# A hybrid attention layer: the compressed branch with queries as the stationary operand, and its values in one block-diagonal product

## The chip, the cores and the metric

The kernel runs on one core of one Trainium2 chip. The metric is the device time of one execution in microseconds. The unchanged kernel took 315.85 us in the median of three executions (315.37 to 315.9). A profiled execution of it took 316.46 us.

## The reference

One decoder layer on 512 tokens of width 1024. After an RMS norm that is modulated by a condition, one projection makes queries, keys, values and gates for two groups of eight heads of width 64. Group A is attention over a window of 128 with a sink per head. Group B (two key groups g, four heads r in each) adds up three branches over the same queries: a compressed one, a selected one and a window of 512. In the compressed branch 31 overlapping blocks of 32 tokens are mapped to one key and one value each, and all 512 queries attend to those that have ended:

```python
def compress_blocks(t, pos, w1, w2):
    ...
    return jax.nn.silu(flat @ w1) @ w2

    logits_c = jnp.einsum('btgrd,bngd->bgrtn', qi, kc)
    p_c = masked_softmax(logits_c, c_end[None, :] <= t[:, None])
    o_cmp = jnp.einsum('bgrtn,bngd->btgrd', p_c, vc)
    ...
o_b = gb[..., 0, :] * o_cmp + gb[..., 1, :] * o_sel + gb[..., 2, :] * o_win
y = concat(o_a * silu(z_a), o_b * silu(z_b)) @ w_out ;  x + gate * y
```

With SEL_TOPK = 16 and only eight blocks of 64, the selected branch takes every earlier block, so it is plain causal attention with its own keys and values.

## The kernel before

Everything is float32 to the outside. A projection is split in a high part (fp32r, which TensorE multiplies in one pass) and the rest (low): three one-pass products high x high, high x low, low x high make one full product. A product of plain float32 operands takes two passes, and each pass shows as a matmul of its own in the profile. The function `split` makes the parts of a weight tile: ScalarE copies the high part (L175), VectorE subtracts (L176). `unit_nat` (L473) projects with tokens on partitions, `unit_col` (L483) with output columns on partitions; a unit of L483 is 24 products of 512 columns, eight steps of three.

Attention of a head pair (g = 0 and 1 with the same r) goes in slots of 128 queries. A slot has scores (L869, or L843 where the first query block takes both branches at once), mask and bias on VectorE (L874, L845), exponential on ScalarE (L881, L850), scaling on VectorE (L902), transposes on TensorE through two PSUM banks called pt (L917, L927), a copy on ScalarE (L918, L928), and the products with values (L944), which collect all four query blocks of one r in one PSUM bank, po. Group A's 16 slots come first, then seven slots for each r of group B. Scores use two PSUM banks called s. The query tiles qs hold high parts in 64 partitions and low parts in the other 64, so a contraction over 128 partitions adds both (L533 on ScalarE, L534 on VectorE).

The compressed branch lies beside that. `cmp_mlp` makes kc and vc (L602 to L648; L631 multiplies the value half). `cmp_attn` makes scores of all queries (L660), with kTc, 32 block keys, as the stationary operand and 512 queries moving: one product for each head, its 32 result rows in one quarter of the PSUM partitions, so that four heads of a group lie in one bank (s for g = 0, pj for g = 1). Since softmax wants queries on partitions, ScalarE copies each bank (L665), TensorE transposes it in four blocks (L669), and VectorE adds the mask (L671). Maximum, subtraction, exponential, sum, gate and scaling follow for two query blocks at a time (L678 to L688). Then the probabilities are transposed back (L695), copied (L697), and `slot_pv` adds for each r and g a product over 32 partitions to the bank po (L950).

What order the engines work in is set by two things. The program writes slots and a stream of side work alternately: `run` advances the stream by a given number of microseconds after each slot, and the stream (`gen1`, `gen2`) yields an estimated cost after each step, between projection steps and between the pieces of `posts`, in which `cmp_mlp` and `cmp_attn` stand. Then a scheduler orders the instructions of each engine by their dependencies and a model of durations. Only what stands in a `block()` keeps its order on TensorE. On the chip each engine runs its own row of instructions in order, so the first that waits holds up all behind it. In `gen2` the side work is eight z units (L483) and four gate slices (L704 on VectorE). The output projection (L483 with yh, yl) ends the program.

Of the kernel before, what the change touches and what calls it, by code (L numbers as in the profile page):

```python
# [81 lines left out]
def hybrid_layer_kernel(ctx, tc, A, out):  # L82
# [31 lines left out]
    rest = con.tile([128, 960], F32, name="rest")  # L114
# [3 lines left out]
    cmask = rest[:, 832:960].rearrange("p (a b) -> p a b", a=NB)  # L118
    qga, kga, qgb, kgs, kgw, kgc = (sml[:, 64 * i:64 * i + 64] for i in range(6))
# [335 lines left out]
    def PT():  # L455
        return ps_t.tile([128, 512], F32, name="pt")
# [40 lines left out]
    qs = {}  # L497
# [96 lines left out]
    def cmp_mlp():  # L594
# [23 lines left out]
        sTv = W2("csTv", (128, 2, 2, 4, 32))  # L618
        ptv = pt[:, 0:256].rearrange("p (c n) -> p c n", c=2)
        ACT.activation(sT, ptv[:, :, 0:64], AF.Copy, scale=0.5)  # L620
        for hc in range(2):
            DVE.tensor_scalar(sTv[:, hc], ptv[:, hc, 64:128].rearrange("p (g n) -> p g n", g=2)[:, :, None, :]
                              .to_broadcast([128, 2, 4, 32]), 0.5, None, op0=OP.mult)
# [5 lines left out]
        for g in range(2):  # L629
            for hc in range(2):  # L630
                PE.matmul(pv[:, 64 * g:64 * g + 64], sTv[:, hc, g].rearrange("p r n -> p (r n)"), w2[:, 1, hc, :],  # L631
                          start=hc == 0, stop=hc == 1)
        for g in range(2):
            vc[g] = mp.tile([128, HD], F32, name=f"vc{g}")
            ACT.activation(vc[g], pv[:, 64 * g:64 * g + 64], AF.Copy)
# [11 lines left out]
        kTc = mp.tile([128, 2, 32], F32, name="kTc")  # L647
        DVE.tensor_copy(kTc.rearrange("p g n -> p (g n)"), pt[:, 0:64])  # L648
# [3 lines left out]
    def cmp_attn():  # L652
        kTc = X["kTc"]
        L = [mp.tile([128, 2, 257], F32, name="pa", bufs=3).rearrange("p a b -> p (a b)")[:, 0:512]
             .rearrange("p (a b c) -> p a b c", a=2, b=2) for _ in range(2)]
        pss = [ps_s.tile([128, 512], F32, name="s"), PJ()]
        with block():
            for g in range(2):
                for r in range(4):
                    PE.matmul(pss[g][32 * r:32 * r + 32, :], kTc[:, g, :], qs[8 + 4 * g + r].bitcast(F32),  # L660
                              start=True, stop=True)
        for g in range(2):
            ps = pss[g]
            st_ = W2("cst")
            ACT.activation(st_.rearrange("p (i q) -> p i q", i=NB), rev(ps.rearrange("p (i q) -> p i q", i=NB)), AF.Copy)  # L665
            yield 0.95
            pt = PT()
            for i in range(NB):
                PE.transpose(pt[:, 128 * i:128 * i + 128], st_[:, 128 * i:128 * i + 128], ident)  # L669
# [435 lines left out]
```

## Time and profile before

| | |
|---|---|
| median of three executions | 315.85 us |
| the profiled execution | 316.46 us |
| its span, first to last instruction | 314.7 us |
| TensorE busy | 306.3 us (97%) |
| VectorE busy | 237.3 us (75%) |
| ScalarE busy | 195.5 us (62%) |
| granted TensorE clock, mean | 0.995 |

A matmul's record lasts from its start to the modelled end of its results, so records of neighbours overlap: 512-wide products start some 0.23 us apart and each is recorded with 0.40 us. What a product costs TensorE is therefore read from the distance of starts, or from the chain of waits, where 18 of them take 4.20 us. The chain follows the work that ended last back to what released it.

### The profile page before, as it was taken

To read this page: it belongs to the slowest core of one execution; us is meant where nothing else is said; L and a number is where in the kernel's file an instruction comes from. 1 tells how busy PE (TensorE), PEld (TensorE's weight loads), DVE (VectorE), ACT (ScalarE), POOL (GpSimd) and SP (SyncE) were. 2 spreads that over 40 slices of the span, in tenths; PEclk is the share of its full clock that TensorE was granted. 3 is DMA by queue.
4 is the path that set the end of the run, shared out by engine and by line. 5 is a ranking of instruction groups with operands and counts; after the bars stand their busy time and mean duration, and the time that the engine had idled before them with its cause. 6 is when DMAs were issued, how large, how long until landed. Compare 5 with 4: busy or idle time off the path is not lost.

```text
span 314.7 us, 5828 instructions
## 1 busy us (share of the span) xinstructions
PE 306.3 (97%) x2122; PEld 252.9 (80%) x2123; DVE 237.3 (75%) x658; ACT 195.5 (62%) x472; POOL 5.1 (2%) x22
## 2 busy tenths in 40 slices
PE   7999999999999999999999999999999999999995
PEld 3678878788988899889873878788788878788885
DVE  5579999999966658898996998988686687544221
ACT  6486448668966674767917767788785877503000
POOL 0000000002000000000000000000000000000000
PEclk9799999999999999999999999999999999999999
DMA  7999948800491809070653004222420220253201
GB/s 268 373 407 409 402 163 253 294 2 0 111 326 26 277 6 277 29 260 2 200 174 130 0 2 133 69 67 70 134 69 0 69 67 3 67 167 109 93 33 69
DMA packets 28232, 44.12 MB, mean 140 GB/s; under 512 B 1787, under 2 KB 19612, under 8 KB 28204
## 3 DMA queue, kind: packets, MB, share of 16 engines
q1 hardware_dynamic: 26908, 41.57, 39.0%
q10 hardware_dynamic: 1296, 2.18, 2.2%
q8 instruction: 17, 0.28, 0.4%
q14 instruction: 11, 0.09, 0.1%
HBM read 41.61 MB, written 2.14 MB: 139 GB/s over the span
## 4 chain that ended last, share of the span: by engine, by line
PE 77%; DVE 12%; DMA 4%; ACT 3%; issue 2%; SPq 0%; POOL 0%; DVEq 0%; ACTq 0%; POOLq 0%
PE pj L483 29%; PE sq L291 7%; PE po L944 7%; PE s L869 7%; PE pj L473 7%; PE pt L927 4%; PE skv L292 4%; DMA raw<-in_w_gate 3%; PE pt L917 3%; PE s L602 3%; DVE qs L534 2%; DVE kTb L552 1%; DVE wl L176 1%; PE po L950 1%; DVE raw L704 1%
## 5 line engine op out<-in xcount | busy, mean ns | idle before, releaser
L175 ACT ACTIVATE wh<-raw 128x512 fp32r<-128x512 f32 (+1 forms) x52 | 31.2, 636 | 13.5 <-PE pj L483 13.4
L176 DVE TENSOR_TENSOR wl<-raw,wh 128x512 fp32r<-128x512 f32 (+1 forms) x52 | 34.8, 690 | 5.2 <-ACT wh L175 3.5
L473 PE MATMUL pj<-wh,hh 128*128 128x256 f32 (+1 forms) x128 | 37.0, 289 | 0.0
L473 PE MATMUL pj<-wl,hh 128*128 128x256 f32 (+1 forms) x128 | 36.7, 287 | 0.1
L473 PE MATMUL pj<-wh,hl 128*128 128x256 f32 (+1 forms) x128 | 36.5, 285 | 0.0
L881 ACT ACTIVATE pp<-pp,nm 128x256 f32<-128x256 f32 (+2 forms) x48 | 29.3, 612 | 6.6 <-DVE nm L874 6.3
L483 PE MATMUL pj<-hh,wh 128*128 128x512 f32 x80 | 32.1, 402 | 0.0
L483 PE MATMUL pj<-hh,wl 128*128 128x512 f32 x80 | 32.0, 400 | 0.0
L483 PE MATMUL pj<-hl,wh 128*128 128x512 f32 x80 | 31.9, 398 | 0.0
L874 DVE CUSTOM_DVE_ANT_0 pp<-s,bias 128x256 f32<-128x256 f32 (+2 forms) x48 | 25.5, 551 | 3.6 <-PE s L869 3.5
L483 PE MATMUL pj<-yl,wh 128*128 128x512 f32 (+1 forms) x72 | 26.6, 372 | 0.0
L483 PE MATMUL pj<-yh,wh 128*128 128x512 f32 (+1 forms) x72 | 26.6, 371 | 0.0
L483 PE MATMUL pj<-yh,wl 128*128 128x512 f32 (+1 forms) x72 | 26.4, 369 | 0.0
L1032 DVE SCALAR_TENSOR_TENSOR fin<-pj,gate,xr 128x512 f32<-128x512 f32 (+1 forms) x9 | 6.2, 691 | 25.1 <-PE pj L483 25.1
L473 PEld LDWEIGHTS pj<-wl,hh 128*128 128x128 f32 x128 | 24.1, 188 | 0.4 <-DVE wl L176 0.3
L473 PEld LDWEIGHTS pj<-wh,hh 128*128 128x128 f32 x128 | 24.1, 188 | 0.3 <-issue 0.2
L473 PEld LDWEIGHTS pj<-wh,hl 128*128 128x128 f32 x128 | 24.1, 188 | 0.2 <-issue 0.2
L869 PE MATMUL s<-kTb,qs 128*128 128x256 f32 (+2 forms) x96 | 23.5, 356 | 0.0
L902 DVE TENSOR_SCALAR pp<-pp,rr,grev 128x256 f32<-128x256 f32 (+2 forms) x48 | 21.1, 476 | 0.7
L928 ACT COPY ptT<-pt 128x384 f32<-128x384 f32 (+1 forms) x32 | 15.7, 531 | 7.0 <-PE pt L927 6.7
L918 ACT COPY ptT<-pt 128x512 f32<-128x512 f32 (+1 forms) x28 | 15.5, 552 | 5.1 <-PE pt L917 4.9
L483 PEld LDWEIGHTS pj<-hh,wh 128*128 128x128 f32 x80 | 15.0, 188 | 3.9 <-issue 1.2
(239 smaller groups left out, 710.3 us busy)
## 6 DMA issues: line engine op xcount, KB each, us to landing
ada_ring<-in_w_ada_rows SPq DMA_DIRECT2D x12, 512.0 KB, 7.4
raw<-in_w_cmp SPq DMA_DIRECT2D x8, 512.0 KB, 5.8
raw<-in_w_gate SPq DMA_DIRECT2D x8, 512.0 KB, 5.9
raw<-in_w_o SPq DMA_DIRECT2D x8, 512.0 KB, 3.7
wst_ring<-in_w_qkv_a SPq DMA_DIRECT2D x8, 384.0 KB, 8.5
xTp<-in_xT SPq DMA_DIRECT2D x8, 256.0 KB, 4.3
bias<-line_d SPq DMA_DIRECT2D x8, 256.0 KB, 3.8
raw<-in_w_q_b SPq DMA_DIRECT2D x4, 512.0 KB, 6.4
```

Source lines behind the costliest of these rows:

```text
L175: ACT.activation(wh, src, AF.Copy)
L176: DVE.tensor_tensor(wl, src, wh.bitcast(F32), op=OP.subtract)
L291: PE.matmul(pj_q[tb], lt, w[:, 0:512], start=f, stop=l, skip_group_check=True)
L473: PE.matmul(bank[:, t * n:(t + 1) * n], h[:, tb * 128:(tb + 1) * 128], w[:, k % 2, :], start=k == 0 and m == 0, stop=k == 7 and m == 2)
L483: PE.matmul(bank, w, h[:, tok], start=k == 0 and m == 0, stop=k == 7 and m == 2)
L869: PE.matmul(ps, qs[h][:, 128 * i:128 * i + 128], k[:, hl_, lo:lo + w], start=hl_ == 0, stop=hl_ == 1)
L874: DVE.tensor_tensor_reduce(out=P[:, g, 0:w], in0=ps, in1=bt, scale=1.0, scalar=init, op0=OP.add, op1=OP.min, accum_out=nm[:, g:g + 1])
L881: ACT.activation(P[:, g, 0:e], P[:, g, 0:e], AF.Exp, bias=nm[:, g:g + 1], scale=-1.0, accum_out=dn[:, g:g + 1])
L902: DVE.tensor_scalar(v, v, rr[:, g:g + 1], gates[:, g, br:br + 1], op0=OP.mult, op1=OP.mult)
L918: ACT.copy(T[:, :, 0:nb, :], rev(pt[:, 0:2 * nb * 128].rearrange("p (g b q) -> p g b q", g=2, b=nb)))
L928: ACT.copy(T[:, 0:nb, :], rev(pt[:, 0:nb * 128].rearrange("p (b q) -> p b q", b=nb)))
L944: PE.matmul(o[64 * g:64 * g + 64, 128 * i:128 * i + 128], vb[:, 64 * g:64 * g + 64], sl["T"][g][:, b, :], start=first_of and b == 0, stop= ...
```

## The change

- **Scores (L660, L665, L669, L671).** The queries become the stationary operand (128 queries by the 128 partitions of high and low parts), the keys move. kTc holds for each g 32 high and 32 low parts of the keys in fp32r, so a product has 64 moving columns and one pass, and its result already has queries on partitions: for each of the four query blocks eight products fill one s bank, ordered (r, g, high or low, 32 keys). VectorE adds the mask to the high half and then the low half. The copies L665 and transposes L669 go, and so does the use of a pj bank. The mask table is reversed along the partitions, because qs holds the queries of a block in reversed order; the gate comes from the reversed gate table (grev), in two products of 8 columns for each pair of blocks.
- **Values (L631, L635, L695, L697, L950).** The value MLP makes both copies of the block values in one product of 64 + 64 stationary columns. `own` masks them to a block-diagonal tile vd, 128 rows (twice two groups of 32 blocks) by 128 columns (two groups of 64), split in a high and a low part vc[0], vc[1]. The probabilities are transposed for two r at a time; for each r the 64 rows of both groups are stored as high part in one half of the partitions and low part in the other (PTc[r]: four ScalarE copies and four VectorE subtractions, for two ScalarE copies before). For each r two one-pass products of 128 rows, 128 columns and 512 queries replace the two two-pass products over 32 rows, one for each g.
- The table `rest` gets two columns, 962 for 960.

```diff
@@ -111,11 +111,12 @@
-    rest = con.tile([128, 960], F32, name="rest")
+    rest = con.tile([128, 962], F32, name="rest")
...
+    own = rest[:, 960:962]
@@ -615,24 +616,25 @@
         for hc in range(2):
             PE.transpose(pt[:, 128 * hc:128 * hc + 128], sh[:, 128 * hc:128 * hc + 128], ident)
         sT = W2("csT", (128, 2, 64))
-        sTv = W2("csTv", (128, 2, 2, 4, 32))
+        sTv = W2("csTv", (128, 2, 2, 64))
         ptv = pt[:, 0:256].rearrange("p (c n) -> p c n", c=2)
         ACT.activation(sT, ptv[:, :, 0:64], AF.Copy, scale=0.5)
         for hc in range(2):
-            DVE.tensor_scalar(sTv[:, hc], ptv[:, hc, 64:128].rearrange("p (g n) -> p g n", g=2)[:, :, None, :]
-                              .to_broadcast([128, 2, 4, 32]), 0.5, None, op0=OP.mult)
+            DVE.tensor_scalar(sTv[:, hc], ptv[:, hc, None, 64:128].to_broadcast([128, 2, 64]), 0.5, None, op0=OP.mult)
         yield 0.25
         po = ps_s.tile([128, 512], F32, name="s")
         for hc in range(2):
             PE.matmul(po[0:64, 0:64], sT[:, hc, :], w2[:, 0, hc, :], start=hc == 0, stop=hc == 1)
         pv = ps_s.tile([128, 512], F32, name="s")
-        for g in range(2):
-            for hc in range(2):
-                PE.matmul(pv[:, 64 * g:64 * g + 64], sTv[:, hc, g].rearrange("p r n -> p (r n)"), w2[:, 1, hc, :],
-                          start=hc == 0, stop=hc == 1)
-        for g in range(2):
-            vc[g] = mp.tile([128, HD], F32, name=f"vc{g}")
-            ACT.activation(vc[g], pv[:, 64 * g:64 * g + 64], AF.Copy)
+        for hc in range(2):
+            PE.matmul(pv[:, 0:64], sTv[:, hc].rearrange("p a n -> p (a n)"), w2[:, 1, hc, :], start=hc == 0, stop=hc == 1)
+        vd = mp.tile([128, 2, HD], F32, name="vd")
+        DVE.tensor_tensor(vd, pv[:, None, 0:64].to_broadcast([128, 2, HD]),
+                          own[:, :, None].to_broadcast([128, 2, HD]), op=OP.mult)
+        for e in range(2):
+            vc[e] = mp.tile([128, 2, HD], F32R, name=f"vc{e}")
+        ACT.activation(vc[0], vd, AF.Copy)
+        DVE.tensor_tensor(vc[1], vd, vc[0].bitcast(F32), op=OP.subtract)
         kcn = mp.tile([64, 2, HD], F32, name="kcn")
         sq = mp.tile([64, HD], F32, name="kcsq")
         ssk = sm.tile([128, 1], F32, name="ssk")
@@ -644,36 +646,32 @@
         yield 1.3
         pt = PT()
         PE.transpose(pt[:, 0:64], kcn.rearrange("p a d -> p (a d)"), ident[0:64, 0:64])
-        kTc = mp.tile([128, 2, 32], F32, name="kTc")
-        DVE.tensor_copy(kTc.rearrange("p g n -> p (g n)"), pt[:, 0:64])
+        kTc = mp.tile([128, 2, 2, 32], F32R, name="kTc")
+        ptk = pt[:, 0:64].rearrange("p (g n) -> p g n", g=2)
+        ACT.activation(kTc[:, :, 0], ptk, AF.Copy)
+        DVE.tensor_tensor(kTc[:, :, 1], ptk, kTc[:, :, 0].bitcast(F32), op=OP.subtract)
         yield 0.1
         X["kTc"] = kTc
 
     def cmp_attn():
         kTc = X["kTc"]
         L = [mp.tile([128, 2, 257], F32, name="pa", bufs=3).rearrange("p a b -> p (a b)")[:, 0:512]
-             .rearrange("p (a b c) -> p a b c", a=2, b=2) for _ in range(2)]
-        pss = [ps_s.tile([128, 512], F32, name="s"), PJ()]
-        with block():
-            for g in range(2):
+             .rearrange("p (i h n) -> p i h n", i=2, n=32) for _ in range(2)]
+        for i in range(NB):
+            ps = ps_s.tile([128, 512], F32, name="s")
+            with block():
                 for r in range(4):
-                    PE.matmul(pss[g][32 * r:32 * r + 32, :], kTc[:, g, :], qs[8 + 4 * g + r].bitcast(F32),
-                              start=True, stop=True)
-        for g in range(2):
-            ps = pss[g]
-            st_ = W2("cst")
-            ACT.activation(st_.rearrange("p (i q) -> p i q", i=NB), rev(ps.rearrange("p (i q) -> p i q", i=NB)), AF.Copy)
+                    for g in range(2):
+                        n = 2 * r + g
+                        PE.matmul(ps[:, 64 * n:64 * n + 64], qs[8 + 4 * g + r][:, 128 * i:128 * i + 128],
+                                  kTc[:, g].rearrange("p e n -> p (e n)"), start=True, stop=True)
+            pv = ps.rearrange("p (h e n) -> p h e n", e=2, n=32)
+            v = L[i // 2][:, i % 2]
+            DVE.tensor_tensor(v, pv[:, :, 0], cmask[:, i:i + 1, :].to_broadcast([128, 8, 32]), op=OP.add)
+            DVE.tensor_tensor(v, v, pv[:, :, 1], op=OP.add)
             yield 0.95
-            pt = PT()
-            for i in range(NB):
-                PE.transpose(pt[:, 128 * i:128 * i + 128], st_[:, 128 * i:128 * i + 128], ident)
-            for i in range(NB):
-                DVE.tensor_tensor(L[i // 2][:, i % 2, g].rearrange("p (r n) -> p r n", r=4),
-                                  pt[:, 128 * i:128 * i + 128].rearrange("p (r n) -> p r n", r=4),
-                                  cmask[:, i:i + 1, :].to_broadcast([128, 4, 32]), op=OP.add)
-            yield 0.44
         for e in range(2):
-            Lv = L[e].rearrange("p i g (r n) -> p (i g r) n", n=32)
+            Lv = L[e].rearrange("p i h n -> p (i h) n")
             m = sm.tile([128, 16], F32, name="cm")
             DVE.tensor_reduce(m, Lv, AX.X, OP.max)
             DVE.tensor_scalar(m, m, -1e25, None, op0=OP.max)
@@ -683,18 +681,25 @@
             DVE.tensor_reduce(dn, Lv, AX.X, OP.add)
             DVE.tensor_scalar(dn, dn, 1e-30, None, op0=OP.max)
             DVE.reciprocal(dn, dn)
-            DVE.tensor_tensor(dn.rearrange("p (i h) -> p i h", i=2), dn.rearrange("p (i h) -> p i h", i=2),
-                              gsig[:, 2 * e:2 * e + 2].rearrange("p i (h c) -> p i h c", c=3)[:, :, :, 0], op=OP.mult)
+            for i in range(2):
+                d = dn[:, 8 * i:8 * i + 8].rearrange("p (r g) -> p r g", g=2)
+                DVE.tensor_tensor(d, d, grev[:, 2 * e + i].rearrange("p (g r c) -> p r g c", g=2, c=3)[:, :, :, 0], op=OP.mult)
             DVE.tensor_tensor(Lv, Lv, dn[:, :, None].to_broadcast([128, 16, 32]), op=OP.mult)
             yield 0.0
         for _ in range(WAIT_L):
             yield 0.0
-        for g in range(2):
+        for p in range(2):
             pt = PT()
             for i in range(NB):
-                PE.transpose(pt[:, 128 * i:128 * i + 128], L[i // 2][:, i % 2, g, :], ident)
-            PTc[g] = T2(F32, f"ptc{g}")
-            ACT.activation(PTc[g], pt, AF.Copy)
+                PE.transpose(pt[:, 128 * i:128 * i + 128], L[i // 2][:, i % 2, 4 * p:4 * p + 4].rearrange("p h n -> p (h n)"),
+                             ident)
+            for n in range(2):
+                r = 2 * p + n
+                PTc[r] = T2(F32R, f"ptc{r}")
+                blocks = lambda ap: ap.rearrange("p (t q) -> p t q", t=NB)
+                high, low, part = blocks(PTc[r][HALF[n], :]), blocks(PTc[r][HALF[1 - n], :]), rev(blocks(pt[HALF[n], :]))
+                ACT.activation(high, part, AF.Copy)
+                DVE.tensor_tensor(low, part, high.bitcast(F32), op=OP.subtract)
             yield 0.44
 
     def gate_slice(q):
@@ -946,9 +951,9 @@
                           skip_group_check=True)
         if i == NB - 1 and br in (0, 2):
             if kind == "b":
-                for g in range(2):
-                    PE.matmul(o[64 * g:64 * g + 64, :], vc[g][32 * r:32 * r + 32, :],
-                              PTc[g][32 * r:32 * r + 32, :], start=False, stop=True, skip_group_check=True)
+                for e in range(2):
+                    PE.matmul(o, vc[e].rearrange("p g d -> p (g d)"), PTc[r], start=False, stop=e == 1,
+                              skip_group_check=True)
             if kind == "a":
                 o_a[r] = T2(F32, f"oa{r}")
                 ACT.activation(o_a[r], o, AF.Copy)
@@ -1071,10 +1076,11 @@
-    t = np.arange(S).reshape(NB, 128).T[:, :, None]
+    t = np.arange(S).reshape(NB, 128).T[::-1, :, None]
+    own = (np.arange(128)[:, None] // 32 % 2 == np.arange(2)[None, :]).astype(np.float32)
...
```

The change also alters the order of rows on the engines. In the rows below, line numbers are those of each kernel: behind the changed part the new file's lines are one to six higher (L483 is L484, L534 L535, L702 the new subtraction for PTc, L791 L796, L803 L808, L874 L879, L845 L850, L902 L907). A row names output<-inputs and the shape; x2 is the number of equal rows in a sequence.

TensorE, from the last value products of group A (L944, L949) on, before:

```order
L944 MATMUL po<-ptT,va 64x128 x14
L660 MATMUL s<-qs_1814,kTc 32x512
L528 MATMUL pt<-first,qn 128x128 x4
L660 MATMUL s<-qs_1854,kTc 32x512
L660 MATMUL s<-qs_2067,kTc 32x512
L483 MATMUL pj<-hl_93,wh 128x512
L483 MATMUL pj<-hh_85,wl 128x512
L660 MATMUL s<-qs_2116,kTc 32x512
L660 MATMUL pj<-qs_1817,kTc 32x512
L660 MATMUL pj<-qs_1857,kTc 32x512
L660 MATMUL pj<-qs_2070,kTc 32x512
L660 MATMUL pj<-qs_2119,kTc 32x512
```

and changed:

```order
L949 MATMUL po<-ptT,va 64x128 x14
L484 MATMUL pj<-hl_93,wh 128x512
L666 MATMUL s<-kTc,qs_1815 128x64
L666 MATMUL s<-kTc,qs_1818 128x64
L666 MATMUL s<-kTc,qs_1855 128x64
L666 MATMUL s<-kTc,qs_1858 128x64
L529 MATMUL pt<-first,qn 128x128 x4
L666 MATMUL s<-kTc,qs_2068 128x64
L484 MATMUL pj<-hh_85,wl 128x512
L666 MATMUL s<-kTc,qs_2071 128x64
L484 MATMUL pj<-hh_78,wh 128x512
L484 MATMUL pj<-hl_86,wh 128x512
```

Before, the eight score products stand close together with two columns (L483) among them. Now six of block 0 stand there, and columns lie between the others: ten columns before the seventh product and seven more behind it, before the eighth. The blocks 1, 2 and 3 of eight products each follow further on.

VectorE at the last query splits (qs), before:

```order
L534 TENSOR_TENSOR qs_2070<-pt,qs_2070 64x512
L898 RECIPROCAL rr<-dn 128x2
L902 TENSOR_SCALAR pp<-pp,rr,grev 128x384 x2
L534 TENSOR_TENSOR qs_2116<-pt,qs_2116 64x512
L176 TENSOR_TENSOR wl<-raw,wh 128x512
L534 TENSOR_TENSOR qs_2119<-pt,qs_2119 64x512
L791 SCALAR_TENSOR_TENSOR sza<-zth,pj 128x512
L874 ISA pp,nm<-s,bias 128x512
```

and changed (sza and yf are the z gate and the gated output of group A, wl a weight split, pa the scores):

```order
L535 TENSOR_TENSOR qs_2071<-pt,qs_2071 64x512
L808 SCALAR_TENSOR_TENSOR yf<-oa_1198,sza 128x512
L903 RECIPROCAL rr<-dn 128x2
L907 TENSOR_SCALAR pp<-pp,rr,grev 128x384
L177 TENSOR_TENSOR wl<-raw,wh 128x512
L535 TENSOR_TENSOR qs_2117<-pt,qs_2117 64x512
L907 TENSOR_SCALAR pp<-pp,rr,grev 128x384
L796 SCALAR_TENSOR_TENSOR sza<-zth,pj 128x512
L535 TENSOR_TENSOR qs_2120<-pt,qs_2120 64x512
L808 SCALAR_TENSOR_TENSOR yf<-oa_1488,sza 128x512
L670 TENSOR_TENSOR pa<-s,rest 128x256
```

The rows sza and yf, which stood behind the last split of qs, now stand ahead of it; another sza stands a little above these rows.

VectorE ahead of the scores of r = 1 (pp, nm), before:

```order
L806 TENSOR_TENSOR yl_2337<-yf,yh_2336 128x512
L176 TENSOR_TENSOR wl<-raw,wh 128x512 x2
L898 RECIPROCAL rr<-dn 128x2
L176 TENSOR_TENSOR wl<-raw,wh 128x512
L902 TENSOR_SCALAR pp<-pp,rr,grev 128x512 x2
L845 ISA pp,nm_2433<-s,bias 128x128
```

and changed (ptc is PTc):

```order
L907 TENSOR_SCALAR pp<-pp,rr,grev 128x512 x2
L702 TENSOR_TENSOR ptc_2416<-pt,ptc_2416 64x512
L796 SCALAR_TENSOR_TENSOR sza<-zth,pj 128x512
L177 TENSOR_TENSOR wl<-raw,wh 128x512
L702 TENSOR_TENSOR ptc_2419<-pt,ptc_2419 64x512
L702 TENSOR_TENSOR ptc_2430<-pt,ptc_2430 64x512
L808 SCALAR_TENSOR_TENSOR yf<-oa_1836,sza 128x512
L796 SCALAR_TENSOR_TENSOR sza<-zth,pj 128x512
L702 TENSOR_TENSOR ptc_2433<-pt,ptc_2433 64x512
L808 SCALAR_TENSOR_TENSOR yf<-oa_2138,sza 128x512
L850 ISA pp,nm_2453<-s,bias 128x128
```

The four subtractions for PTc stand directly ahead of these scores, with two sza and two yf rows among them that stood behind. On TensorE 46 columns now stand between the value products with vs for r = 0 and the scores L843 (now L848) of r = 1, with the eight transposes of the probabilities among them; before, eight columns stood there.

More of the change, by code (lines that the diff above doesn't have):

```diff
@@ L1073, in _layout @@
     w2 = np.stack([g("w_cmp_k2")[0].reshape(2, 128, 64), g("w_cmp_v2")[0].reshape(2, 128, 64)]).transpose(2, 0, 1, 3)
-    t = np.arange(S).reshape(NB, 128).T[:, :, None]
+    t = np.arange(S).reshape(NB, 128).T[::-1, :, None]
+    own = (np.arange(128)[:, None] // 32 % 2 == np.arange(2)[None, :]).astype(np.float32)
     cmask = np.where(16 * np.arange(32)[None, None, :] + 31 <= t, 0.0, -BIG).astype(np.float32)
     a["rest"] = cc(np.concatenate([np.broadcast_to(smalls, (128, 416)), eye[::-1], pos.reshape(128, -1),
-                                   w2.reshape(128, -1), cmask.reshape(128, -1)], axis=1))
+                                   w2.reshape(128, -1), cmask.reshape(128, -1), own], axis=1))
     dist = NEAR // 2 - 1 - np.arange(NEAR)
```

## The prediction

> **What bounds the kernel now.** I read the shares of the page first, then the chain of waits in order of time, then the busy times by stretch. The page's lines:
>
> ```profile
> span 314.7 us, 5828 instructions
> PE 306.3 (97%) x2122; PEld 252.9 (80%) x2123; DVE 237.3 (75%) x658; ACT 195.5 (62%) x472; POOL 5.1 (2%) x22
> PE 77%; DVE 12%; DMA 4%; ACT 3%; issue 2%; SPq 0%; POOL 0%; DVEq 0%; ACTq 0%; POOLq 0%
> ```
>
> TensorE is busy in 97% of the span and carries 77% of the chain. The chain in order of time shows where it carries all of it:
>
> ```profile
> 170.15 0.70 DVE qs L534
> 170.90 1.04 PE pj L660 x2
> 171.94 0.59 PE pt L917 x4
> ...
> 194.47 0.47 PE s L843 x4
> ...
> 270.32 41.20 PE pj L483 x200
> 311.54 0.48 DVE fin L1032
> ```
>
> The last link on another engine is the high/low split of a query tile (qs, L534), for which the compressed scores (L660) wait. From 170.90 to 311.52 every link is TensorE. So a microsecond of TensorE work less after 171 is a microsecond off the end, as long as nothing else makes TensorE wait. Whether something could, the busy times by stretch say (columns: window, length, then busy time and count on PE, PEld, DVE, ACT, POOL, then clock, DMA share, GB/s):
>
> ```profile
> 172.00:194.50 22.50, 22.50 (x156) 18.92 (x157) 21.14 (x63) 15.57 (x36) 0.00 (x0) 1.00 0.12 40
> 204.00:225.40 21.40, 21.39 (x180) 17.32 (x180) 18.26 (x63) 16.95 (x49) 0.00 (x0) 1.00 0.24 75
> 225.40:252.40 27.00, 27.00 (x205) 22.22 (x207) 18.71 (x63) 19.79 (x52) 0.00 (x0) 1.00 0.19 60
> 252.40:270.30 17.90, 17.85 (x157) 13.86 (x157) 11.70 (x34) 11.21 (x28) 0.00 (x0) 1.00 0.10 31
> ```
>
> The first row is the stretch of the compressed softmax, and there VectorE is busy in 21.14 of 22.50 us (94%). It is not the bound only because TensorE has projection columns (L483) to run meanwhile. The other rows are the passes of r=1, 2 and 3, each up to its L950; there VectorE has 3.1, 8.3 and 6.2 us free.
>
> **The scores, on TensorE.** TensorE's timeline where they run:
>
> ```profile
> 166.01 1.05 PE L660 MATMUL s<-qs,kTc 128*32 128x512 f32 x2
> 166.98 0.66 PE L528 MATMUL pt<-first,qn 128*128 128x128 f32 x4
> 167.57 1.05 PE L660 MATMUL s<-qs,kTc 128*32 128x512 f32 x4
> 168.55 0.50 PE L483 MATMUL pj<-hl,wh 128*128 128x512 f32 x1
> 168.89 0.40 PE L483 MATMUL pj<-hh,wl 128*128 128x512 f32 x1
> 169.45 0.62 PE L660 MATMUL s<-qs,kTc 128*32 128x512 f32 x1 [0.16 <-DVE qs L534]
> 169.46 0.63 PE L660 MATMUL pj<-qs,kTc 128*32 128x512 f32 x3
> 170.90 1.04 PE L660 MATMUL pj<-qs,kTc 128*32 128x512 f32 x2 [0.38 <-DVE qs L534]
> ```
>
> Each product is two matmuls (two passes). Products that are ready together run side by side in strips of 32 columns, and a group takes 0.98 us (167.57 to 168.55) whether one, two or four are in it. They come as 1, 2, 4 and 1, since the queries arrive late. From 166.01 to 171.88 pass 5.87 us; the transposes take 0.59 of it (166.98 to 167.57) and the two columns 2 x 0.233, by the row of 18 of them in these rows of the chain:
>
> ```profile
> 108.09 0.84 PE s L631 x8
> ...
> 178.74 0.44 PE pt L927 x4
> ...
> 196.61 4.20 PE pj L483 x18
> ...
> 204.07 1.00 PE po L950 x4
> 205.08 0.59 PE pt L917 x4
> ```
>
> So the scores with their waits cost 5.87 - 0.59 - 0.47 = 4.81 us. After the change they are 32 products with 128x128 stationary operand and 64 moving columns, one pass each. The trace has that form in the value half of the MLP (L631, 128x64): 0.84 us for eight, 0.105 each, so 3.36 us. The upper bound comes from the nearest one-pass form, with 128 moving columns:
>
> ```profile
> 68.39 0.41 PE L869 MATMUL s<-kT,qs 128*128 128x128 f32 x2 [0.35 <-ACT qs L533]
> L869 PE MATMUL s<-kT,qs 128*128 128x128 f32 x16 | 3.3, 287 | 0.7 <-ACT qs L533 0.3 <-DVE nm L874 0.3
> ```
>
> Two take 0.41 and a single one 0.28, so they start 0.13 apart; 32 of that are 4.2 us. The queries come no earlier, so I expect the two waits (0.16 + 0.38) to stay: 3.36 + 0.54 - 4.81 = **-0.9**, bounds -1.45 (no wait) and -0.1 (0.13 and the waits).
>
> **Transposes of scores.** The eight of L669 go; four of the same form take 0.44 (L927 above): **-0.87**.
>
> **Values.** L950 takes 1.00 us for each r. Two full one-pass 512-wide products take 2 x 0.233 = 0.47. Four times 0.53 is **-2.1**; at the low end the switch from 64-column to full tiles costs 0.15 in each, as the first transposes behind L950 show (0.59 against 0.44 for four), so -1.5.
>
> **MLP values.** Eight matmuls of L631 become four: **-0.42**, at 108 us, where TensorE is busy too. All four are TensorE work: **-4.3**, bounds -2.9 and -4.85.
>
> **What VectorE and ScalarE get.** The rows that price it (line, operation, tiles, shape, count | busy us, mean ns):
>
> ```profile
> L671 DVE TENSOR_TENSOR pa<-pt,rest 128x128 f32<-128x128 f32 x8 | 1.8, 280 | 0.0
> L612 DVE SCALAR_TENSOR_TENSOR csh<-cth,s 128x256 f32<-128x256 f32 x1 | 0.4, 421 | 2.4 <-ACT cth L610 2.4
> L534 DVE TENSOR_TENSOR qs<-pt,qs 64x512 fp32r<-64x512 f32 x16 | 11.0, 687 | 1.4 <-ACT qs L533 1.0
> L686 DVE TENSOR_TENSOR cd<-cd,gsig 128x16 f32<-128x16 f32 x2 | 0.3, 170 | 0.0
> L533 ACT ACTIVATE qs<-pt 64x512 fp32r<-64x512 f32 x16 | 9.5, 593 | 13.7 <-PE pt L528 8.1 <-DVE qs L534 5.4
> L697 ACT ACTIVATE ptc<-pt 128x512 f32<-128x512 f32 x2 | 1.1, 596 | 1.3 <-PE pt L695 1.3
> L665 ACT ACTIVATE cst<-s 128x512 f32<-128x512 f32 x1 | 0.6, 592 | 0.0
> ```
>
> Mask and sum: eight passes of 128x256 (0.421) for eight of 128x128 (0.280), +1.1 us. Low halves of the four stacked probability tiles: 4 x 0.687 = +2.75. The gate product: four for two, +0.3. Together VectorE gets +4.2 us in its densest stretch. ScalarE loses two score copies (2 x 0.59) and its two probability copies become four (+2 x 0.59): nothing. The small extra operations on keys and values at 109 to 111 us are some 0.3 us on each engine and lie under projection columns, so they cost nothing; uncovered, they would add that 0.3 us. The two more columns of the constants' load are 8 bytes a partition, nothing.
>
> **Whether TensorE can cover it.** In the changed order VectorE runs two more 128x512 rows (sza) ahead of the last query split, and one (yf) in a place where it now idles for 0.73 us:
>
> ```profile
> 167.61 0.17 DVE L898 RECIPROCAL rr<-dn 128x2 f32<-128x2 f32 x1 [0.73 <-ACT pp L881]
> ```
>
> By the 0.6 us between two such rows, shown further down, that split ends about 1.2 us later. TensorE meanwhile runs 18 columns between the first and the last score product of block 0. From 166.01 that is 0.23 + 8 x 0.105 + 0.44 + 18 x 0.233 = 5.7 us, to 171.7, against 170.85 + 1.2 = 172.0 on VectorE. Then VectorE has to go to its first L845 row of r=1. How fast it goes through 128x512 rows stands here:
>
> ```profile
> 194.74 0.29 DVE L845 CUSTOM_DVE_ANT_0 pp<-s,bias 128x128 f32<-128x128 f32 x1 [0.91 <-PE s L843]
> 195.59 0.69 DVE L176 TENSOR_TENSOR wl<-raw,wh 128x512 fp32r<-128x512 f32 x1
> 196.20 0.68 DVE L791 SCALAR_TENSOR_TENSOR sza<-zth,pj 128x512 f32<-128x512 f32 x1
> ```
>
> Before, 170.85 to 194.74 is 23.9 us, about 21.4 of them work. The order adds the 4.2 us and moves three more rows (one yf, two wl) ahead, 0.6 each: 27.4, to 199.4. TensorE needed 171.88 to 194.47 = 22.6 us to its L843 rows of r=1; now add 24 score products (2.5), take off the transposes (0.87), and add 12 columns (62 stand there in the changed order, 50 in the old; +2.8): 27.0, to 199.0 with the waits. A tie: each microsecond that VectorE idles makes TensorE wait, because the low halves (L702 of the changed kernel) also free the two pt banks: behind a transpose that waits for a bank stand in TensorE's queue the scores L843 of r=1, and for those VectorE waits in turn. VectorE idled 6% of this stretch, 1.6 us of 27.4; I take **+1.2** (0 to 1.6). The columns spent there are missing later: 23 instead of 51 in the pass of r=2, 22 for 24 in r=1, and 17 for 16 in r=3. The r=2 pass would last 27.0 - 28 x 0.233 - 0.53 = 19.9 us, with some 2.8 us of column splits less on each of VectorE and ScalarE (six columns use one split tile, 0.6 us): about 80 to 85% busy, as in r=1 now. I add **+0.3** (0 to 1).
>
> **Sum.** -4.3 + 1.2 + 0.3 = -2.8 us. The profiled execution took 316.46 (span 314.7 and 1.8 around), which gives 313.7; it lies 0.6 above the median of 315.85, so the median should come to **313.0**. Its own range, from the bounds, is 311.5 to 314.6.
>
> **Rivals.** (1) VectorE's extra work costs nothing, because columns cover all of it: -4.3 to -4.85, **311.3**. For it: the changed order has columns at each place where TensorE waits now. Against: the tie above.
>
> (2) The swap of the scores loses. Packed in fours, a product costs 0.98/4 = 0.245 us, eight 1.96, so the 32 narrow ones (3.36) cost 1.4 more, if the rest of the 4.81 is waiting for queries that comes back. Sum -4.3 + 0.9 + 1.4 + 1.5 = -0.5: **315.3**. The Trainium skill (TensorEngine Tiling (Array Packing), Performance Considerations) speaks for it: for a 32-wide side it recommends swapping it in as the stationary operand with four column tiles, which is what the kernel does now. The trace agrees only for the one group of four; the others came as 1, 2 and 1 and filled 0.98 each. Against it: TensorE no longer stands there, it has 18 columns between.
>
> (3) Slower: the columns spent early are missing in the pass of r=2. If its slots are paced by the softmax's round over VectorE and ScalarE and still need 26.5 us (27.0 - 0.5) instead of 19.9, the 28 missing columns turn into 6.6 us of waiting: 313.0 + 6.6 - 0.3 = 319.3; halfway 316.2. It decides from a pass of about 23.0 us on (19.9 + 0.3 + 2.8). Against it: r=3 needs 17.9 us with 16 columns, so the round itself is no longer than that.
>
> **Chances.** Forecast 0.55, (1) 0.2, (2) 0.12, (3) 0.1, others 0.03. Range **311.0 to 315.6**: up from below (1) to past (2), leaving (3) out. What a measurement of this kernel can tell from no change is 0.2%, 0.6 us. Faster: 0.55 + 0.2 + 0.04; same: most of (2) and a little of (3), 0.09; slower: 0.12.
>
> **What would show it.** Score products of 64 columns some 0.105 us apart; no two-pass pair of 32 rows at L950's place but two products in 0.47 us; four low halves of 0.69 us on VectorE; TensorE reaching L843 of r=1 near 200 (now 194.5), but the end of r=3's values near 267.5 (now 270.3); the r=2 pass at 20 us. It is wrong if a one-pass product of 64 columns takes over 0.2 us (+3 us), if TensorE waits over 3 us for VectorE between 165 and 205, or if the r=2 pass stays above 23 us.

## The result: 311.65 us, ahead of the forecast

| | before | changed |
|---|---|---|
| median of the executions beside each other | 317.61 us (315.37 to 321.44, six) | 311.65 us (311.18 to 312.03, six) |
| ratio | | 0.9863, 95% interval 0.9828 to 0.9898 |
| profiled execution | 316.46 us, span 314.7 | 312.03 us, span 309.4 |

One thing is needed to read these times: in some executions of most versions TensorE's clock is granted at half rate for 3.4 or about 10 us, from 11 us on, which costs some 1.2 or 4 us, so a time below without an interval is the median of the executions whose mean granted clock was 0.997 or more, and the ratios and intervals are over wider sets, so they are not the quotients of the medians shown.

By that measure the kernel before takes 315.3, 315.4 and 315.6 us in three sets of executions on two chips. The changed kernel takes 311.65 in a set whose chip is not on record: 3.7 to 4.0 us less, where 2.8 were forecast (313.0, range 311.0 to 315.6). It is the time of rival (1).

A time also holds what passes outside the span from the first to the last instruction: 1.8 to 1.9 us in the medians of the other versions, but 2.25 us in that of the changed kernel (1.8 to 2.6, and 2.6 in the profiled execution). By spans the kernel before takes 313.5 to 313.7 us and the changed one 309.4, which is 4.1 to 4.3 us less. Where the changed kernel is compared with other versions below, the spans (medians of the same executions) are given too.

The same views of the changed kernel. Its line numbers have moved by a few: score products are L666, low halves L702, values L955, projection columns L484. First the page's busy times:

```profile
PE 302.0 (98%) x2119; PEld 255.2 (82%) x2119; DVE 241.6 (78%) x666; ACT 194.9 (63%) x472; POOL 4.1 (1%) x22
```

TensorE is busy for 4.3 us less and VectorE for 4.3 us more, as forecast (-4.3 and +4.2). Some 0.5 us of TensorE's figure lies ahead of all that was changed, where the profile of before has the half clock for a while. From the first products of the compressed MLP (99.49 and 98.60 us in the chains below) to the last step, TensorE is busy for 206.4 us instead of 210.2 and idle for 1.3 instead of 1.8. The chain of waits (start, length, engine, tile and line):

```profile
98.60 3.67 PE s L603 x32
...
136.09 1.68 PE po L949 x28
...
173.42 0.81 PE s L666 x8
...
197.64 0.69 PE s L848 x4
...
206.44 0.67 PE po L955 x2
207.12 0.44 PE pt L922 x4
...
226.96 0.67 PE po L955 x2
...
247.27 0.67 PE po L955 x2
...
263.65 0.66 PE po L955 x2
264.31 41.95 PE pj L484 x204
...
306.28 0.48 DVE fin L1037
```

Its counterparts of before that are not shown yet are these:

```profile
99.49 3.67 PE s L602 x32
...
137.42 1.68 PE po L944 x28
...
225.36 1.00 PE po L950 x4
...
252.38 1.00 PE po L950 x4
...
269.31 1.00 PE po L950 x4
```

Set side by side, the chains show where the time went:

| place | before | changed | changed - before |
|---|---|---|---|
| compressed MLP, first products | 99.49 | 98.60 | -0.89 |
| values of group A | 137.42 | 136.09 | -1.33 |
| values of r=0 | 204.07 | 206.44 | +2.37 |
| values of r=1 | 225.36 | 226.96 | +1.60 |
| values of r=2 | 252.38 | 247.27 | -5.11 |
| values of r=3 | 269.31 | 263.65 | -5.66 |
| last columns begin | 270.32 | 264.31 | -6.01 |
| last step | 311.54 | 306.28 | -5.26 |

The first 0.89 us stand ahead of all that was changed: they are the half clock early in the profile of before (the last section has its rows). The change itself is worth 5.26 - 0.89 = 4.4 us in this pair of profiles. Up to r=0 the changed kernel is behind, because it runs more columns there; it has them back in the pass of r=2, which lasts 20.3 us (226.96 to 247.27) for 27.0 before. At the end stand 204 columns for 200, and four columns are 0.93 us.

Whether VectorE held TensorE up, the stretch from 164 us to the values of r=0 tells (columns as in the prediction's windows). Before:

```profile
164.00:204.00 40.00, 39.45 (x286) 30.03 (x284) 36.12 (x109) 29.16 (x71) 0.00 (x0) 1.00 0.23 76
```

Changed:

```profile
164.00:206.40 42.40, 42.36 (x299) 35.63 (x295) 41.31 (x115) 29.94 (x72) 0.00 (x0) 1.00 0.23 71
```

VectorE works 41.31 of 42.40 us (97%, 90% before), and by the records TensorE stands still for 0.04 us (0.55 before). No stall took the place of what was removed.

### The profile page after: what moved, and what is told of

Same layout as the page of the kernel before. It is cut to its first block, busy times and chain, and to the rows that moved or that the text cites. A ratio compares the mean times of both kernels' runs of the same rounds, so it can differ in the third digit from the quotient of the medians.

```text
span 309.4 us, 5849 instructions
## 1 busy us (share of the span) xinstructions
PE 302.0 (98%) x2119; PEld 255.2 (82%) x2119; DVE 241.6 (78%) x666; ACT 194.9 (63%) x472; POOL 4.1 (1%) x22
## 4 chain that ended last, share of the span: by engine, by line
PE 78%; DVE 11%; ACT 4%; DMA 3%; issue 1%; SPq 1%; DVEq 0%; ACTq 0%
PE pj L484 28%; PE po L949 8%; PE sq L292 8%; PE pj L474 8%; PE s L874 7%; PE pt L932 4%; PE skv L293 4%; PE pt L922 3%; PE s L603 3%; DVE qs L535 2%; DMA raw<-in_w_gate 2%; DVE raw L709 2%; DMA xTp<-in_xT 2%; DVE wl L177 1%; PE s L666 1%
## 5 line engine op out<-in xcount | busy, mean ns | idle before, releaser
L484 PE MATMUL pj<-hl,wh 128*128 128x512 f32 x80 | 32.2, 402 | 0.0
L484 PE MATMUL pj<-hh,wl 128*128 128x512 f32 x80 | 32.0, 400 | 0.0
L484 PE MATMUL pj<-hh,wh 128*128 128x512 f32 x80 | 32.0, 400 | 0.0
L879 DVE CUSTOM_DVE_ANT_0 pp<-s,bias 128x256 f32<-128x256 f32 (+2 forms) x48 | 25.6, 553 | 4.1 <-PE s L874 3.6
L484 PE MATMUL pj<-yh,wl 128*128 128x512 f32 (+1 forms) x72 | 26.6, 370 | 0.0
L484 PE MATMUL pj<-yl,wh 128*128 128x512 f32 (+1 forms) x72 | 26.6, 369 | 0.0
L484 PE MATMUL pj<-yh,wh 128*128 128x512 f32 (+1 forms) x72 | 26.4, 371 | 0.0
L874 PE MATMUL s<-kTb,qs 128*128 128x256 f32 (+2 forms) x96 | 24.3, 356 | 0.0
L907 DVE TENSOR_SCALAR pp<-pp,rr,grev 128x256 f32<-128x256 f32 (+2 forms) x48 | 21.0, 475 | 0.5
L534 ACT ACTIVATE qs<-pt 64x512 fp32r<-64x512 f32 x16 | 9.5, 592 | 13.4 <-PE pt L529 7.3
L484 PEld LDWEIGHTS pj<-hh,wh 128*128 128x128 f32 x80 | 15.1, 188 | 3.0 <-issue 0.2
```

Source lines behind the costliest of these rows:

```text
L484: PE.matmul(bank, w, h[:, tok], start=k == 0 and m == 0, stop=k == 7 and m == 2)
L874: PE.matmul(ps, qs[h][:, 128 * i:128 * i + 128], k[:, hl_, lo:lo + w], start=hl_ == 0, stop=hl_ == 1)
L879: DVE.tensor_tensor_reduce(out=P[:, g, 0:w], in0=ps, in1=bt, scale=1.0, scalar=init, op0=OP.add, op1=OP.min, accum_out=nm[:, g:g + 1])
L907: DVE.tensor_scalar(v, v, rr[:, g:g + 1], gates[:, g, br:br + 1], op0=OP.mult, op1=OP.mult)
```

## Experiments

### Each half of the change alone

The first run has the new scores with the old values, the second the old scores with the new values. Cut to the core, the first against the changed kernel:

```diff
-                for e in range(2):
-                    PE.matmul(o, vc[e].rearrange("p g d -> p (g d)"), PTc[r], start=False, stop=e == 1,
-                              skip_group_check=True)
+                for g in range(2):
+                    PE.matmul(o[64 * g:64 * g + 64, :], vc[g][32 * r:32 * r + 32, :],
+                              PTc[g][32 * r:32 * r + 32, :], start=False, stop=True, skip_group_check=True)
```

and the second:

```diff
-                    for g in range(2):
-                        n = 2 * r + g
-                        PE.matmul(ps[:, 64 * n:64 * n + 64], qs[8 + 4 * g + r][:, 128 * i:128 * i + 128],
-                                  kTc[:, g].rearrange("p e n -> p (e n)"), start=True, stop=True)
+                    PE.matmul(pss[g][32 * r:32 * r + 32, :], kTc[:, g, :], qs[8 + 4 * g + r].bitcast(F32),
+                              start=True, stop=True)
```

Expected of the scores alone:

> Only the scores are changed: queries stationary, keys in high and low parts, mask added in two passes, the score copies and transposes gone; probabilities and values stay as before, with two-pass products over 32 rows (the copy of the probabilities turns the order of the queries back). If the gain is TensorE work that went (theory), this is worth 4.81 - 32 x 0.101 - 0.2 of waiting = -1.4 us for the scores and -0.87 for the transposes, together -2.3 us (ratio 0.993). If packing the scores in strips was as cheap and what went was only waiting for queries (rival), it is worth the transposes alone, -0.9 us (0.997), or less.

Expected of the values alone:

> Only the values are changed: block-diagonal high and low tiles, stacked probabilities, two one-pass products for each r, the MLP values in one product; the scores stay as before with their copies and transposes. Theory (TensorE work): 4 x (1.00 - 0.67) + 0.45 = -1.8 us (ratio 0.994), although VectorE gets four low halves more (2.75 us) in its densest stretch. Rival (VectorE's extra work ends on the path): -1.8 + 2.7 = +0.9 us, or no change.

Measured: scores alone 313.6 us, ratio 0.9963 (0.9929 to 0.9998); values alone 312.9, ratio 0.9926 (0.9892 to 0.9960); the kernel before on that chip 315.3. That is -1.7 and -2.4, together -4.1, and both at once gave -3.7 to -4.0 (by spans -1.7, -2.45 and -4.1 to -4.3). So the halves add up, and little or none of the gain is lost between them. Against the two expectations the scores fell 0.6 us short of -2.3 and the values went 0.6 past -1.8. The values' expectation had left out that the rows behind them get cheaper too, some 0.15 us for each r. The scores' had left out that columns behind narrow products start later, which makes 0.3 of its 0.6; the rest is open. Both figures are worked out further down. The sizes are those of the prediction's terms: -0.9 - 0.87 = -1.8 for scores and their transposes, -2.1 - 0.42 = -2.5 for the values.

### The low halves that VectorE got

What do the 2.75 us of L702 cost? In one run ScalarE writes zeros in their place, so that the low part of the probabilities is left out of the computation; in another each is subtracted twice.

```diff
                 ACT.activation(high, part, AF.Copy)
-                DVE.tensor_tensor(low, part, high.bitcast(F32), op=OP.subtract)
+                ACT.activation(low, part, AF.Copy, scale=0.0)
```

```diff
-                DVE.tensor_tensor(low, part, high.bitcast(F32), op=OP.subtract)
+                for _ in range(2):
+                    DVE.tensor_tensor(low, part, high.bitcast(F32), op=OP.subtract)
```

Expected of the first:

> The changed kernel with the four low halves of the probabilities written by ScalarE as zeros (a copy with factor 0) and not subtracted by VectorE: 2.75 us less on VectorE, 2.4 us more on ScalarE; it leaves out the low part of the compressed probabilities. If VectorE's extra work is covered (theory), the time stays that of the changed kernel, 311.7 within 0.4 us (ratio to before 0.986). If VectorE at 99% in this stretch costs time (rival, the forecast's 1.2 us), it falls by 1 to 2.7 us, to 309.0 to 310.6 (0.979 to 0.983).

Expected of the second:

> The changed kernel with each low half of the probabilities subtracted twice, 2.75 us more on VectorE in its densest stretch, where it idled 0.3 us in 25. If the columns that stand ready on TensorE cover it with room to spare (theory), under +0.5 us on the changed kernel's 311.7 (ratio to before up to 0.988). If the two engines are at a tie there (rival, as in the forecast's sum), +1.5 to +2.75 us, 313.2 to 314.4 (0.992 to 0.996).

Measured: without them 311.7 us, ratio 0.9887 (0.9832 to 0.9942), the changed kernel's own time (span 309.9 for 309.4). Since TensorE waits 0.4 us for the zeros of ScalarE in the trace of this run, a gain of that size could be hidden, but the 1 to 2.7 us of the rival could not. The low halves are covered. Doubled: 312.9, ratio 0.9913 (0.9880 to 0.9947), 1.3 us more (1.6 by spans) for 2.75 us of VectorE. That is more than the theory and no more than the low end of the rival, and most of the price is not paid where the work stands. The end of the chain of that run:

```profile
267.50 0.68 PE po L956 x2
...
268.20 1.89 DVE yf L809 x3
...
271.95 35.92 PE pj L484 x177
```

TensorE's timeline there, with the idle time and its releaser in brackets:

```profile
270.71 0.97 PE L484 MATMUL pj<-yh,wh 128*128 128x512 f32 x3 [0.68 <-ACT yh L811]
271.95 0.50 PE L484 MATMUL pj<-yl,wh 128*128 128x512 f32 x1 [0.27 <-DVE yl L812]
```

The order kept TensorE busy in the dense stretch by running columns there. Behind the last values are left eight columns (from 268.00 on), these three and the 177: 188 for the changed kernel's 204, 16 x 0.233 = 3.7 us of cover spent early. The last columns then come before VectorE has finished their operands, and TensorE waits 0.95 us in these two rows. The remaining 0.4 us or so are not traced to a place. In this kernel cover is one store for the whole program: VectorE's work is free until the columns run short, and the bill comes at the end.

### The old scores, written late

If the lateness of the queries was the loss of the old packed products, and not the shape, writing the old products five steps later should bring as much as the swap:

```diff
+        for _ in range(5):
+            yield 0.0
         pss = [ps_s.tile([128, 512], F32, name="s"), PJ()]
         with block():
             for g in range(2):
```

This went alone into the kernel before, and into the version with the new values alone. Expected of the former:

> The kernel before, with the packed score products written some steps later, so that all eight queries are ready when the first of them is due and the eight stand next to each other in TensorE's queue. Nothing else is changed. Theory (what the old form lost was waiting for operands: groups of one, two and four took 0.98 us alike): two groups of four, 2 x 0.98 = 1.96 us for 4.81, so -2.85 us at the most and -2 us with something lost elsewhere: 0.991 to 0.994 of the kernel before. Rival (the gain of the swap lies in the shape of the products themselves): no change, 0.998 to 1.002. Third way (the softmax now comes later and the probabilities are late for the values of r=0): slower, up to 1.01.

Expected of the latter:

> The new values alone, with the old packed scores written as late as in the run before. Theory: -2.4 us for the values (the run with the values alone) and -2 to -2.85 for two full groups of scores: -4.4 to -5.3 us, 0.983 to 0.986, as good as the changed kernel (0.986) or up to 1 us better, since 1.96 of scores and 0.87 of transposes are 0.5 less than 3.36. Rival (swapping the operands is better than packing them): as the values alone, 0.992.

Measured on one chip with the kernel before at 315.4: alone 312.8 us, ratio 0.9870 (0.9815 to 0.9924), -2.5, inside the theory's range. The chain shows the eight products in two full groups:

```profile
174.38 1.00 PE s L662 x8
175.37 0.86 PE pj L662 x8
176.23 0.59 PE pt L671 x4
```

The scores take 1.85 us, from 174.38 to 176.23, for 4.81 before. The old form, moved to where its operands are ready, gains more (-2.5) than the swap at the old place (-1.7). With the new values it gave 309.9 us in the one execution out of six whose clock was full throughout (ratio 0.9877, 0.9802 to 0.9952, over all of them): 5.4 below the kernel before, at the edge of what was expected, and 1.7 below the changed kernel (1.3 by spans).

### A bank of scores put back where it was

The changed kernel no longer holds a pj bank for scores. Is that what lets columns run between the score products?

```diff
-            ps = ps_s.tile([128, 512], F32, name="s")
+            ps = PJ() if i == 0 else ps_s.tile([128, 512], F32, name="s")
```

> The changed kernel, with the scores of the first query block in a pj bank in place of an s bank, so that one of the two banks of the projection columns is held while the scores wait for the last queries, as in the kernel before. Theory (the freed bank is what lets TensorE run columns between the score products): the waits of some 0.5 us and the loss of columns come back, 0.5 to 2 us over the changed kernel, 0.988 to 0.992 of the kernel before. Rival (the bank plays no part): as the changed kernel, 0.986.

Measured: 311.05 us, ratio 0.9811 (0.9744 to 0.9878). That is not slower; by the medians it is 0.6 us faster than the changed kernel, but by spans only 0.2 (309.2 for 309.4). In its trace the columns still stand between the score products, and TensorE is idle for 0.2 us from 164 us to the values of r=0. The theory falls: the bank plays no part that could be seen.

### The new scores, written late too

The same two lines in the changed kernel, beside a second run of the new values with late packed scores:

```diff
+        for _ in range(5):
+            yield 0.0
         for i in range(NB):
             ps = ps_s.tile([128, 512], F32, name="s")
```

> The changed kernel, with its 32 narrow score products written as late as in the two runs with late packed products, so that all queries are ready for them too. It differs from the new values with late packed scores in the form of the scores alone. Theory (the packed form is the cheaper one once its groups are full: 1.86 us from 174.38 to 176.23 and 0.87 of transposes, 2.73, against 32 x 0.105 and a switch, 3.5; the changed kernel loses 0.7 us by waits for late queries): 0.5 to 0.9 us under the changed kernel's 311.6, 310.7 to 311.2, and 0.6 to 1.2 us above the new values with late packed scores. Rival (lateness brought all of it and the form is indifferent): as the packed ones, 309.9 within 0.3.

> The new values with late packed scores once more, beside the run above on one chip, since five of the six executions before had the slow start. Theory: 309.9 where the clock is granted in full from the start, 1.7 us under the changed kernel and 5.4 under the kernel before. Rival (the single undisturbed execution was a lucky one): 310.7 or more, no better than the changed kernel with late scores.

Measured, the kernel before at 315.6: late swapped scores 310.5 us, ratio 0.9824 (0.9779 to 0.9870); the late packed ones 310.2 in four executions, ratio 0.9849 (0.9791 to 0.9908). Both are over 1 us faster than the changed kernel (0.7 and 1.0 by spans, 308.7 and 308.4 for 309.4). The single 309.9 before was the low end of a spread, here 309.97 to 310.65. Expected between the two forms were 0.6 to 1.2 us (theory) or none within 0.3 (rival); 0.3 came out, no more than the executions of one form differ among themselves. The two profiles say more: from the first products of the MLP to the last step the swapped form takes 206.41 us and the packed one 206.39.

```profile
98.98 3.67 PE s L603 x32
...
305.39 0.48 DVE fin L1039
```

```profile
98.68 3.67 PE s L603 x32
...
305.07 0.48 DVE fin L1042
```

TensorE is busy for 205.4 and 205.3 us of these. So the form of the scores does not matter here once the operands are there, and the 0.8 us that the expectation counted as less TensorE work did not show; where it went stays open.

What the delay does shows in the chain. In the changed kernel the chain runs over VectorE ahead of the scores:

```profile
162.20 1.20 DVE raw L709
...
167.97 0.69 DVE qs L535
169.01 1.71 PE pj L484 x7
```

With the delay the same stretch is TensorE's throughout, and the first group is whole:

```profile
162.99 1.68 PE po L951 x28
...
167.64 2.79 PE pj L484 x12
...
173.00 0.96 PE s L668 x8
```

## Why the prediction was right, and which step failed

**The terms on TensorE were right.** A group of eight score products takes 0.81 us, 0.101 each, for the 0.105 taken from the MLP. The waits for queries (0.54) were expected to stay, and did so only in part. This is the answer on the query splits of the changed kernel (first and last start; then who waited for them, us and times):

```profile
L535 DVE TENSOR_TENSOR qs<-pt,qs x16: 673/685/694, 63.5 to 169.8; 64x512 fp32r<-64x512 f32 x16
...
  PEld s L666: 0.7, 2
```

Only the loads of the stationary operand (PEld), which run beside products, still wait. The two waits of the products themselves, 0.16 and 0.38 us before, are gone from the records; by the starts some 0.2 us is left, ahead of the seventh product of block 0:

```profile
168.27 0.40 PE L484 MATMUL pj<-hh,wh 128*128 128x512 f32 x1
168.71 0.30 PE L666 MATMUL s<-kTc,qs 128*128 128x64 f32 x1
168.84 0.48 PE L484 MATMUL pj<-hl,wh 128*128 128x512 f32 x1
169.16 0.40 PE L484 MATMUL pj<-hh,wl 128*128 128x512 f32 x1
```

A column that follows narrow products holds TensorE for 0.32 us (168.84 to 169.16) where one behind another column takes 0.233; that happens three times. So the scores cost 2.4 us for three full groups, 0.9 for block 0, 0.2 of waiting and 0.3 of such columns, 3.8 in all: -1.0 for the -0.9 forecast. The size came out right, but its second part was not the wait that the prediction had named.

The values took 0.67 us for the 0.47 forecast, but the transposes behind them went from 0.59 to 0.44 (r=0). Values and switch together fell from 1.59 to 1.11, 0.48 for each r: -1.9 for the -2.1 forecast. The halves alone (-1.7 and -2.4) confirm the sums.

**VectorE's load was right too.** The forecast counted 27.4 us from the last query split to the first row of r=1, and a tie with TensorE. The last split starts at 169.8 and takes 0.7; it ends 0.5 us later than before, the early half clock taken off, for the 1.2 forecast. The row of r=1 is this one of VectorE's timeline, 28.0 us behind that end, of which VectorE worked 27.6:

```profile
198.46 0.29 DVE L850 CUSTOM_DVE_ANT_0 pp<-s,bias 128x128 f32<-128x128 f32 x1
```

TensorE reaches the scores for it at 197.64; the forecast's 199.0, less the 0.89 of the early half clock, is 198.1.

**The step that failed** is the term +1.2: "VectorE idled 6% of this stretch, 1.6 us of 27.4; I take +1.2". It took idle time of before for a rate at which VectorE loses time. But that idle time was VectorE waiting for TensorE and ScalarE. The groups of before from 164 to 204 us (behind the last bar the idle time and its releasers):

```profile
L874 DVE CUSTOM_DVE_ANT_0 pp<-s,bias 128x384 f32<-128x384 f32 x6 | 3.2, 551 | 0.5 <-PE s L869 0.5
...
L791 DVE SCALAR_TENSOR_TENSOR sza<-zth,pj 128x512 f32<-128x512 f32 x4 | 2.7, 682 | 0.8 <-ACT zth L789 0.8
L874 DVE CUSTOM_DVE_ANT_0 pp<-s,bias 128x512 f32<-128x512 f32 x4 | 2.7, 684 | 0.7 <-PE s L869 0.7
...
L898 DVE RECIPROCAL rr<-dn 128x2 f32<-128x2 f32 x6 | 0.9, 158 | 0.7 <-ACT pp L881 0.7
...
L845 DVE CUSTOM_DVE_ANT_0 pp<-s,bias 128x128 f32<-128x128 f32 x4 | 0.9, 288 | 0.9 <-PE s L843 0.9
```

And of the changed kernel, where VectorE idles 1.1 us in all:

```profile
L879 DVE CUSTOM_DVE_ANT_0 pp<-s,bias 128x384 f32<-128x384 f32 x6 | 3.1, 554 | 0.0
...
L796 DVE SCALAR_TENSOR_TENSOR sza<-zth,pj 128x512 f32<-128x512 f32 x3 | 2.1, 688 | 0.0
...
L903 DVE RECIPROCAL rr<-dn 128x2 f32<-128x2 f32 x6 | 1.0, 160 | 0.0
...
L850 DVE CUSTOM_DVE_ANT_0 pp<-s,bias 128x128 f32<-128x128 f32 x4 | 0.9, 287 | 0.0
```

The 3.6 us of waiting in these groups are gone from the stretch; only its end still has 0.4 us of a wait of that kind, ahead of the L903 row at 206.90. The more work VectorE has, the later it asks, and the less it waits for the others. The prediction itself quoted two of these releasers (0.91 for L843, 0.73 for L881). TensorE stood still for 0.04 us, and the run without the low halves is no faster. Without the +1.2 the sum is -4.0; the medians say -3.7 to -4.0, the spans -4.1 to -4.3, the two profiles -4.4.

**The range** held by its width. The forecast of 313.0 rested on a stall that did not come, and 311.65 lies at the range's low end, which had been drawn to take in rival (1): that the number fell inside is no proof of the mechanism. The "own range, from the bounds" of 311.5 to 314.6 does not follow from the bounds given: they add up to -4.85 and to -2.9 + 1.6 + 1.0 = -0.3, which is 311.0 to 315.6.

**The pass of r=2** was forecast at 19.9 us and 0.3 of waits, and measured 20.3. Rival (3), missing columns there, is ruled out: 23.0 us were needed. What it feared is real, but somewhere else and for a larger load: the doubled low halves made the columns run out at the very end.

**Rival (1)**, full cover, is what happened; it said 311.3, and 311.65 was measured. The prediction had given it a chance of 0.2.

**Rival (2)**, the swap loses, is wrong for this change, since the scores alone gain 1.7. Its arithmetic was right in part: eight packed products in full groups take 1.85 us, and it had said 1.96. Its forecast that the rest of the 4.81 is waiting was right as well. The sentence of the Trainium skill that stood beside it (TensorEngine Tiling (Array Packing), Performance Considerations: for a 32-wide side, swap it to be stationary and pack four column tiles) agrees with the rows of the late packed run, 1.85 us and 1.03 of transposes (0.59 and 0.44) for 32 x 0.101 = 3.2 of narrow products; in the time of the two late forms the difference does not show. What neither the prediction nor that sentence weighed is the order: the packed form was slow because it was asked for before its operands. With the new values, the swap is 1.2 us better at the old place (311.65 for 312.9; 1.6 by spans), and no better at the late one (310.5 for 310.2).

## What to carry to other kernels

Idle time of an engine that waits for the bounding engine is no loss rate: give it more work and the waiting goes first, so charge a stall only where the added work passes the time at which the other engine asks. Count the cover (here projection columns) over the whole program, since extra work that is hidden in one stage is paid where the cover runs out. And before a product is given another form, look whether its groups were full: moving it to where its operands are ready can be worth more than the form, and two lines of delay were worth 0.7 (by spans) to 1.1 us here on top of the change.

## What the runs showed of the hardware

**Narrow products are not cheap in proportion to their columns.** With a 128x128 stationary operand each, products of 64 moving columns take 0.101 us in a row and transposes of 128 take 0.109 (0.44 for four), while 512 columns take 0.233: an eighth of the columns costs 0.43 of the time. The Trainium skill (TensorE: Matmul & The Clock Gate, LDWEIGHTS) prices a load by its columns over 1.2 GHz, 107 ns for 128; the 101 to 105 ns here agree with a load as the limit, which no run tested by itself.

**The clock can be held at half for different times at the same place.** The mean granted clock stands behind POOL's count. Before:

```profile
10.00:12.00 2.00, 2.00 (x20) 1.23 (x18) 1.09 (x6) 0.52 (x2) 0.00 (x0) 0.83 1.05 403
12.00:16.00 4.00, 3.53 (x27) 1.77 (x21) 2.15 (x14) 1.38 (x3) 0.00 (x0) 0.66 1.03 404
```

Changed:

```profile
10.00:12.00 2.00, 1.75 (x18) 1.24 (x18) 1.09 (x4) 0.80 (x2) 0.00 (x0) 1.00 1.02 394
```

And the new values with late packed scores, first run:

```profile
12.00:16.00 4.00, 3.53 (x23) 1.51 (x25) 1.80 (x12) 0.61 (x2) 0.00 (x0) 0.50 1.04 408
16.00:24.00 8.00, 8.00 (x42) 5.30 (x41) 5.45 (x10) 4.68 (x9) 0.00 (x0) 0.67 0.99 379
```

The same kernel had 314.5 us with the long half clock and 309.9 without: 4.6 us, more than the whole change.

**A plain float32 product cost about as much as four one-pass products here, not two.** A score product of before shows as two matmul records. Standing alone it filled 0.98 us with its 512 moving columns, where one fp32r product of 512 columns takes 0.233. Only the packing of four into strips brought it back to a quarter of that.
